# Two token tiles in one PSUM bank in a projection chunk of 256 columns of a decoder step

## The chip, the cores and the metric

The kernel runs on one core of a Trainium2 chip. Its time is device time in microseconds for one execution of the whole program, two decoder layers. The engines are TensorE (PE, matmuls and transposes into PSUM), ScalarE (ACT), VectorE (DVE), GpSimd (POOL, which here also issues the indirect DMAs, the gathers) and SyncE (SP, which issues the other DMAs). PSUM is held as eight banks of 128 partitions by 512 fp32 words.

## The reference

One step of a two-layer decoder for 512 prompt tokens and for 64 tokens of eight samples that have a paged cache. Each layer projects the input once, gives the columns to three groups of heads, and ends in a feed-forward block:

```python
def layer(x, pos, past, w, lam_init, past_len):
    z = x @ w['w_in']
    ca, cg, nq, ck, cv, sk, sv, wk, wv, gt, dq, dk, dv = jnp.split(z, _split_points(), axis=-1)
    ...
    y_conv, new_conv = conv_mixer(ca, cg, conv_buf, ...)
    ...
    o_nsa = gate[0] * o_cmp + gate[1] * o_sel + gate[2] * o_win
    ...
    o_diff = diff_mixer(dq, dk_all, dv_all, pos, dk_pos, lam, w['diff_subln_g'], lam_init)
    mix = jnp.concatenate([y_conv, o_nsa, o_diff], axis=-1) @ w['w_out']
    x = layer_norm(DN_ALPHA * x + mix, w['ln1_g'], w['ln1_b'])
    h = jax.nn.silu(x @ w['ffn_w1']) * (x @ w['ffn_w3'])
    return layer_norm(DN_ALPHA * x + h @ w['ffn_w2'], w['ln2_g'], w['ln2_b']), ...
```

The columns that matter here are `nq` (the queries of the sparse attention, 512 columns) and `dv` (the values of the differential attention, 256 columns), the last two chunks that a layer projects. (Lines marked "..." and the arguments of the mixers are cut.)

## The kernel before

The 576 tokens lie as four prompt tiles of 128 tokens and one samples' tile of 64. Matrices are kept as a high and a low part, and a product is the sum of three matmuls (high by high, high by low, low by high; `product`, L358). For the samples' tile high and low parts are stacked as 128 rows, so it takes two matmuls and one addition of its two halves afterwards.

`chunk` (L558) projects N columns of `w_in` at a time through `dense_tok` (L374). A chunk reads `w_in` in eight weight tiles kt of 128 rows: load by SP (L181), split into high and low by ACT (L187) and DVE (L190), then the five token tiles m. Weight tiles 0 to 5 run as steps in which all five token tiles are served; the last two are kept, and token tile by token tile is finished with them and handed on: samples first, then prompt tiles 0 to 3. Each token tile sums up in a PSUM bank of its own. The banks go by tags, of which there are a fixed number (`PBUFS`, L148): a0 and a1 two each, t1 two, h one and t0 one:

```python
acc = [PS(b) for b in ("a0", "a0", "a1", "a1", last)]
...
for m in (4, 0, 1, 2, 3) if last == "t0" else range(5):
```

In a chunk `last` is "t0": the samples' tile lies in the one bank t0. When a token tile is done, `evac` (L559) copies it from PSUM into an H slot (`cp`, L213, in this stage on ACT) and calls the chunk's sink. `sink_q` (L636) rotates the queries and transposes them on PE (L649) through bank t0. `sink_e` (L591) copies the values with POOL (L593) and stores them.

The chunks run in the order d, c, q, e (`ORDER`), so the chunk of `dv`, called e here, follows the queries' chunk. It has N = 256; the others have 512 or 280. Beside them run the operands of the differential attention (`diff_operands`, L852, transposes L866) and parts of the samples' branch (`spe`, L1103 to L1124). After the chunks come the prompts' attention (`diff_scores`, L872, whose scores sum up in bank a0; `diff_turn`, L891) and the samples' (`keys_T`, L1142, transposes of gathered keys; `sample_diff_av`, L1281, products with gathered values; L985 and L1214 are transposes of attention weights).

Working tiles come from 30 U slots and 26 H slots; `W` gives the one that was freed longest ago, and a load into a slot waits for its last reader. The program is written as streams that `merge` (L124) deals out by planned costs, and a list scheduler then sets the order on each engine by its own estimate of times and by what each instruction depends on. So a dependency that changes can move instructions far from it.

Of the kernel before, what the change touches and what calls it, by code (L numbers as in the profile page):

```python
# [135 lines left out]
def kernel(ctx: ExitStack, tc: tile.TileContext, a: dict, o: dict, nlayers: int = DEPTH):  # L136
# [27 lines left out]
    def free(*ts, lag=0):  # L164

        for t in ts:
            _, tag, i = owner.pop(id(t))
            since[tag][i] = next(clock) + lag

    def T(tag, shape, dt=F):  # L170
        return sb.tile(shape, dt, tag=tag, name=f"{tag}_{next(uid)}", bufs=1)
# [5 lines left out]
    def PS(tag, dt=F):  # L177
        return ps.tile([128, 512], dt, tag=tag, name=f"{tag}_{next(uid)}", bufs=PBUFS[tag])

    def load(out, in_):  # L180
        nc.sync.dma_start(out, in_)  # L181
# [4 lines left out]
    def act(out, in_, func=AF.Copy, **kw):  # L186
        S.activation(out, in_, func, **kw)  # L187
# [13 lines left out]
    def split(h, l, x, eng=None):  # L201

        act(h, x)
        return sub(l, x, h.bitcast(F), eng)
# [8 lines left out]
    def cp(out, in_):  # L213

        if next(turn) % ratio[0] == 1:
            return V.tensor_copy(out, in_)  # L216
        return S.activation(out, in_, AF.Copy)  # L217
# [8 lines left out]
    def mm(out, lhsT, rhs, start, stop):  # L226
        return PE.matmul(out, lhsT, rhs, start=start, stop=stop)  # L227

    def wait_for(ins, *others):

        for x in others:
            tc.add_manual_dep(ins.ins, x.ins.name, mybir.DependencyInfo(mybir.DependencyClass.Sync, mybir.DependencyReason.DATA), reason="together")
# [8 lines left out]
    first = T("first", [128, NFIRST])  # L241
# [120 lines left out]
    def product(out, s_, wh, wl, first, last):  # L362


        if not isinstance(s_, tuple):
            mm(out, s_, wh, first, False)
            mm(out, s_, wl, False, last)
        else:
            hs, ls = s_
            mm(out, hs, wh, first, False)  # L370
            mm(out, hs, wl, False, False)
            mm(out, ls, wh, False, last)

    def dense_tok(w_rows, KT, N, st, sink, tail=0, last="h", done=None, raws=None, nh=8):  # L374


        acc = [PS(b) for b in ("a0", "a0", "a1", "a1", last)]

        def weights(kt, wh, wl):
            if raws and kt in raws:  # L380
                raw = raws[kt]
            else:
                raw = W("H", [128, N])
                load(raw, w_rows(kt))
            split(wh, wl, raw)
            free(raw)

        def step(kt, m, wh, wl):
            first, last = kt == 0, kt == KT - 1
            out = acc[m][:, :N]  # L390
            product(out, st(kt, m), wh, wl, first, last)

        for kt in range(KT - tail):
            wh, wl = own = [W("H", [128, N], FR) for _ in range(2)]
            weights(kt, wh, wl)
            for m in range(5):
                step(kt, m, wh, wl)
            free(*own)
            if done:
                done(kt)  # L400
            yield N * 14 / 2400
        res = []
        for kt in range(KT - tail, KT):
            if len(res) < nh:
                own = [W("H", [128, N], FR) for _ in range(2)]
                wh, wl = own
            else:
                own = [W("U", [128, 2, N], FR)]
                wh, wl = own[0][:, 0], own[0][:, 1]
            weights(kt, wh, wl)  # L410
            res.append((kt, wh, wl, own))
        for m in (4, 0, 1, 2, 3) if last == "t0" else range(5):
            for kt, wh, wl, _ in res:
                step(kt, m, wh, wl)
            sink(m, acc[m])
            yield 0.6 + N * len(res) * 2.8 / 2400
        for kt, _, _, own in res:
            free(*own)
            if done:
                done(kt)  # L420
# [34 lines left out]
    def layer(l, x, x_src, raws):  # L455
# [100 lines left out]
            return tuple(x[part][kt // 2][:, kt % 2, c0:c0 + R] for part in range(2))  # L556

        def chunk(c0, N, sink, raws=None):  # L558
            def evac(m, acc):  # L559
                z = W("H", [128 if m < 4 else NS, N])  # L560
                if m < 4:
                    cp(z, acc[:, :N])
                    sink(m, 128, z)
                else:
                    act(z, acc[64:128, :N])
                    add(z, acc[0:64, :N], z)
                    sink(m, NS, z)
                free(z, lag=LAG)

            yield from dense_tok(lambda kt: w_in[kt * 128:(kt + 1) * 128, c0:c0 + N], 8, N, st_x, evac, tail=TAIL, last="t0", raws=raws, nh=NH)  # L570
# [933 lines left out]
        for kt in range(8):  # L1504
            small = kt < 3
            parts = [[W("H", [128, 512], FR) for _ in range(2)] if small else W("U", [128, D], FR) for _ in range(2)]
            for c in range(2):
                wh, wl = (t[c] if small else t[:, c * 512:(c + 1) * 512] for t in parts)
# [6 lines left out]
        st = st_of(mix)  # L1515
        ln.fetch(0)
        for m in range(5):
            if m < 4:
                ln.fetch(m + 1)
            acc = [PS("a0"), PS("a1")]  # L1520
# [48 lines left out]
        for c in range(2):  # L1569
            def sink(m, acc):  # L1570
                ln.add(m, c, acc)
                if c:
                    ln.finish(m)
# [61 lines left out]
```

## Time and profile before

| | us |
|---|---|
| median of 3 runs | 2069.74 |
| lowest and highest | 2063.65 and 2074.16 |
| the profiled execution, its own time | 2071.4 |
| its span | 2069.6 |

The page of the profile gives the busy time of each engine and its share of the span; the trace behind it has every instruction with its start, its duration and what ended the idle time ahead of it. A row of a timeline reads: start, duration, engine, line, operation, output tile <- input tiles, shape, number of instructions taken together, and in brackets the idle time just before and what released the engine. In names of tiles, a, t and h are PSUM banks (a0 and a1 both read a), H and U are slots, `in_...` are tensors in DRAM, and `first` is the identity that PE transposes by. The mean granted clock of PE is 0.969 of full speed over the run.

### The profile page before, as it was taken

To read this page: it belongs to the slowest core of one execution; us is meant where nothing else is said; L and a number is where in the kernel's file an instruction comes from. 1 tells how busy PE (TensorE), PEld (TensorE's weight loads), DVE (VectorE), ACT (ScalarE), POOL (GpSimd) and SP (SyncE) were. 2 spreads that over 40 slices of the span, in tenths; PEclk is the share of its full clock that TensorE was granted. 3 is DMA by queue.
4 is the path that set the end of the run, shared out by engine and by line. 5 is a ranking of instruction groups with operands and counts; after the bars stand their busy time and mean duration, and the time that the engine had idled before them with its cause. 6 is when DMAs were issued, how large, how long until landed. Compare 5 with 4: busy or idle time off the path is not lost. (4 is left out here: it accounts for less than half of the span.)

```text
span 2069.6 us, 32882 instructions
## 1 busy us (share of the span) xinstructions
PE 1933.5 (93%) x12222; PEld 1631.7 (79%) x12222; DVE 1101.2 (53%) x3012; ACT 916.7 (44%) x2368; POOL 206.7 (10%) x233
## 2 busy tenths in 40 slices
PE   8999888989999999999999997989899999999997
PEld 6887765656689999988879776656566899999885
DVE  3568476866573333323456665678666633333236
ACT  3635565767422333321245545667673223333211
POOL 2011022121010000000120110221110000000002
PEclk9999899999999999999999998999999999999999
DMA  6423143243423332352153321441433332324411
GB/s 200 137 76 103 28 145 128 83 146 99 136 92 117 97 122 83 93 187 77 48 174 108 96 71 45 152 155 57 138 108 118 112 122 82 122 84 130 149 56 51
DMA packets 190252, 223.91 MB, mean 108 GB/s; under 512 B 19092, under 2 KB 138812, under 8 KB 189948
## 3 DMA queue, kind: packets, MB, share of 16 engines
q1 hardware_dynamic: 171660, 154.69, 24.5%
q0 software_dynamic: 18432, 67.12, 10.2%
q8 instruction: 97, 1.59, 0.3%
q14 instruction: 63, 0.52, 0.1%
HBM read 206.23 MB, written 24.15 MB: 111 GB/s over the span
## 5 line engine op out<-in xcount | busy, mean ns | idle before, releaser
L227 PE MATMUL a<-H,U 128*128 128x512 f32 (+3 forms) x2264 | 552.8, 411 | 14.0 <-ACT H L187 11.6
L190 DVE TENSOR_TENSOR H<-H,H 128x512 fp32r<-128x512 f32 (+5 forms) x392 | 255.5, 657 | 510.5 <-ACT H L187 482.8
L227 PEld LDWEIGHTS a<-H,U 128*128 128x128 f32 (+1 forms) x2264 | 386.2, 190 | 111.2 <-issue 15.4
L187 ACT ACTIVATE H<-H 128x512 fp32r<-128x512 f32 (+4 forms) x418 | 240.8, 583 | 519.9 <-DMA H<-in_ffn_w_dram 298.8
L227 PE MATMUL a<-U,H 128*128 128x288 f32 (+2 forms) x3008 | 399.2, 306 | 7.9 <-DMA U<-in_cache_diff_v_dram,idx 6.7
L227 PEld LDWEIGHTS a<-U,H 128*128 128x128 f32 (+1 forms) x3008 | 370.2, 181 | 21.7 <-DMA U<-in_cache_diff_v_dram,idx 7.3
L227 PE MATMUL t<-U,H 128*128 128x288 f32 x1584 | 288.7, 297 | 0.4 <-ACT U L187 0.4
L227 PEld LDWEIGHTS t<-U,H 128*128 128x128 f32 x1584 | 243.5, 190 | 1.0 <-ACT U L187 0.6
L227 PE MATMUL a<-U,U 128*128 128x512 f32 (+4 forms) x744 | 200.7, 379 | 7.9 <-ACT H L187 3.7
L227 PE MATMUL h<-U,U 128*128 128x257 f32 (+5 forms) x708 | 152.4, 376 | 13.1 <-ACT U L217 13.0
L217 ACT ACTIVATE U<-t 64x256 f32<-64x256 f32 (+4 forms) x393 | 142.8, 366 | 45.6 <-PE t L757 24.5
L227 PEld LDWEIGHTS a<-U,U 128*128 128x128 f32 x744 | 129.4, 191 | 34.2 <-ACT U L187 7.4
L227 PEld LDWEIGHTS h<-U,U 128*128 128x128 f32 (+1 forms) x708 | 114.6, 185 | 40.3 <-ACT U L217 17.3
L227 PE MATMUL h<-U,H 128*128 128x288 f32 x528 | 140.9, 296 | 0.0
L187 ACT ACTIVATE U<-H 128x288 fp32r<-128x288 f32 (+4 forms) x160 | 64.4, 438 | 143.8 <-DVE H L190 104.1
L217 ACT ACTIVATE H<-t 128x512 f32<-128x512 f32 (+1 forms) x172 | 94.9, 564 | 45.6 <-PE t L1145 23.5
L547 DVE SCALAR_TENSOR_TENSOR U<-U,cw,U 128x512 f32<-128x512 f32 x240 | 109.4, 510 | 0.1
L227 PEld LDWEIGHTS h<-U,H 128*128 128x128 f32 x528 | 99.3, 188 | 0.0
L190 POOL TENSOR_TENSOR U<-U,U 128x512 f32<-128x512 f32 x24 | 33.6, 1417 | 599.1 <-DVE rs_u L321 459.9
L187 ACT ACTIVATE U<-t 128x256 fp32r<-128x256 f32 (+4 forms) x132 | 47.1, 370 | 97.0 <-PE t L350 40.8
L190 DVE TENSOR_TENSOR U<-H,U 128x64 fp32r<-128x64 f32 (+6 forms) x204 | 69.9, 385 | 31.1 <-ACT U L187 24.8
L216 DVE COPY H<-t 128x512 f32<-128x512 f32 (+1 forms) x92 | 57.2, 626 | 45.7 <-PE t L1214 15.6
(293 smaller groups left out, 2268.9 us busy)
## 6 DMA issues: line engine op xcount, KB each, us to landing
H<-in_ffn_w_dram SPq DMA_DIRECT2D x264, 256.0 KB
H<-in_w_in_dram SPq DMA_DIRECT2D x64, 256.0 KB
H<-in_w_out_dram SPq DMA_DIRECT2D x32, 256.0 KB
xd<-U SPq DMA_DIRECT2D x24, 256.0 KB
U<-xd SPq DMA_DIRECT2D x12, 512.0 KB
U<-in_x_prompt_dram SPq DMA_DIRECT2D x8, 512.0 KB
H<-in_state_nsa_win_v_dram SPq DMA_DIRECT2D x16, 256.0 KB
H<-in_state_nsa_win_k_dram SPq DMA_DIRECT2D x16, 256.0 KB
```

The lines of the kernel that those rows point to most:

```text
L187: S.activation(out, in_, func, **kw)
L190: return (eng or V).tensor_tensor(out, x, y, op=op)
L216: return V.tensor_copy(out, in_)
L217: return S.activation(out, in_, AF.Copy)
L227: return PE.matmul(out, lhsT, rhs, start=start, stop=stop)
L547: V.scalar_tensor_tensor(out=ac, in0=ex, scalar=wc, in1=ac, op0=OP.mult, op1=OP.add)
```

## The change

It concerns chunks with 2N <= 512, and that is chunk e alone, once in each layer. Its four prompt tiles lie two in a bank: tiles 0 and 1 in the two halves of the first a0, tiles 2 and 3 in those of the second. The samples' tile takes a bank a1; bank t0 and the other a1 are not used by this chunk any more. The flag that starts a sum is set for the first tile of a bank only, and the second tile's first matmul is made to come after it. The copies of a pair are made after the last matmul of the pair's second tile. Nothing else is written differently; every instruction stays, and in each layer 16 matmuls, one ACT and one DVE instruction name an a bank where they named t.

```diff
--- before.py
+++ after.py
@@ -363,18 +363,24 @@
 
 
         if not isinstance(s_, tuple):
-            mm(out, s_, wh, first, False)
-            mm(out, s_, wl, False, last)
+            i = mm(out, s_, wh, first, False)
+            j = mm(out, s_, wl, False, last)
         else:
             hs, ls = s_
-            mm(out, hs, wh, first, False)
+            i = mm(out, hs, wh, first, False)
             mm(out, hs, wl, False, False)
-            mm(out, ls, wh, False, last)
+            j = mm(out, ls, wh, False, last)
+        return i, j
 
     def dense_tok(w_rows, KT, N, st, sink, tail=0, last="h", done=None, raws=None, nh=8):
 
 
-        acc = [PS(b) for b in ("a0", "a0", "a1", "a1", last)]
+        if 2 * N > 512:
+            acc = [PS(b) for b in ("a0", "a0", "a1", "a1", last)]
+        else:
+            acc = [t[:, c * 256:(c + 1) * 256] for t in (PS(b) for b in ("a0", "a0", "a1")) for c in range(2)]
+
+        starts = {}
 
         def weights(kt, wh, wl):
             if raws and kt in raws:
@@ -386,9 +392,15 @@
             free(raw)
 
         def step(kt, m, wh, wl):
-            first, last = kt == 0, kt == KT - 1
+
+            first, last = kt == 0 and (2 * N > 512 or m % 2 == 0), kt == KT - 1 and (2 * N > 512 or m in (1, 3, 4))
             out = acc[m][:, :N]
-            product(out, st(kt, m), wh, wl, first, last)
+            i, j = product(out, st(kt, m), wh, wl, first, last)
+            if 2 * N <= 512 and kt == 0:
+                if m % 2:
+                    wait_for(i, starts[m - 1])
+                starts[m] = i
+            return j
 
         for kt in range(KT - tail):
             wh, wl = own = [W("H", [128, N], FR) for _ in range(2)]
@@ -411,8 +423,13 @@
             res.append((kt, wh, wl, own))
         for m in (4, 0, 1, 2, 3) if last == "t0" else range(5):
             for kt, wh, wl, _ in res:
-                step(kt, m, wh, wl)
-            sink(m, acc[m])
+                j = step(kt, m, wh, wl)
+            if 2 * N > 512 or m == 4:
+                sink(m, acc[m])
+            elif m % 2:
+
+                sink(m - 1, acc[m - 1], j)
+                sink(m, acc[m])
             yield 0.6 + N * len(res) * 2.8 / 2400
         for kt, _, _, own in res:
             free(*own)
@@ -556,10 +573,12 @@
             return tuple(x[part][kt // 2][:, kt % 2, c0:c0 + R] for part in range(2))
 
         def chunk(c0, N, sink, raws=None):
-            def evac(m, acc):
+            def evac(m, acc, after=None):
                 z = W("H", [128 if m < 4 else NS, N])
                 if m < 4:
-                    cp(z, acc[:, :N])
+                    i = cp(z, acc[:, :N])
+                    if after:
+                        wait_for(i, after)
                     sink(m, 128, z)
                 else:
                     act(z, acc[64:128, :N])
```

The scheduler gives another order. In the chunk e of layer 0, on PE (a is the bank of a token tile, H_482 to H_497 the halves of a weight tile, high and low; U_24 to U_30 the prompts' x, U_32 the samples'), the samples' products of weight tiles 0 to 3 (H_484 to H_494) stood behind prompt tile 0's of weight tile 4 (H_496, H_497) before:

```order
L227 MATMUL a_482_2569<-H_493_2631,U_29_123 128x256
L227 MATMUL a_479_2566<-H_496_2651,U_26_120 128x256
L227 MATMUL a_479_2566<-H_497_2652,U_26_120 128x256
L227 MATMUL a_479_2566<-H_496_2651,U_30_124 128x256
L227 MATMUL t_483_2570<-H_484_2571,U_32_126 128x256
L227 MATMUL t_483_2570<-H_485_2572,U_32_126 128x256
L227 MATMUL t_483_2570<-H_487_2591,U_32_126 128x256
L227 MATMUL t_483_2570<-H_488_2592,U_32_126 128x256
L227 MATMUL t_483_2570<-H_490_2611,U_32_126 128x256
```

and now stand with the weight tile that they belong to:

```order
L227 MATMUL a_480_2567<-H_482_2569,U_24_118 128x256
L227 MATMUL a_480_2567<-H_483_2570,U_24_118 128x256
L227 MATMUL a_480_2567<-H_482_2569,U_28_122 128x256
L227 MATMUL a_481_2568<-H_483_2570,U_32_126 128x256
L227 MATMUL a_479_2566<-H_485_2589,U_24_118 128x256
L227 MATMUL a_480_2567<-H_485_2589,U_24_118 128x256
L227 MATMUL a_481_2568<-H_485_2589,U_32_126 128x256
L668 MATMUL t_444_2388<-first_63,H_439_2370 128x128 x4
L885 MATMUL t_477_2554<-first_63,U_472_2535 128x128 x4
```

The samples' products of the first weight tile have moved ahead of those of the second weight tile, and so on for each.

Some 75 instructions later, on PE, the transposes of the gathered keys of sel_k (L1145, in the new file L1164) and a score of 512 columns (a_612, now a_610). Before:

```order
L866 MATMUL t_568_2916<-first_63,U_562_2885 128x128 x4
L227 MATMUL a_612_3047<-U_474_2541,U_473_2540 128x512
L227 LDWEIGHTS ident_b_103
L227 MATMUL a_612_3047<-causal_b_105,ident_b_103 128x128
L895 MATMUL t_576_2939<-first_63,H_518_2768 128x128
L1145 MATMUL t_545_2833<-first_63,U_539_2821 128x128 x4
L1145 MATMUL t_547_2840<-first_63,U_540_2823 128x128 x4
```

and now:

```order
L885 MATMUL t_566_2914<-first_63,U_560_2883 128x128 x4
L1164 MATMUL t_543_2831<-first_63,U_537_2819 128x128 x4
L1164 MATMUL t_545_2838<-first_63,U_538_2821 128x128 x4
L227 MATMUL a_610_3045<-U_474_2541,U_473_2540 128x512
L227 LDWEIGHTS ident_b_103
L227 MATMUL a_610_3045<-causal_b_105,ident_b_103 128x128
L914 MATMUL t_574_2937<-first_63,H_516_2766 128x128
```

The transposes of keys have moved ahead of the score. On POOL the gather for the first of them (U_539, now U_537) has moved ahead of the last of the three copies of `sink_e` before it.

In layer 0, among the gathers that POOL issues in the attention, before (U_1139 and U_1140 are the pair of gathers of diff_v that `sample_diff_av` uses together):

```order
L313 DMA U_1119_4876<-in_cache_diff_v_dram,idx_15_92 128x1024
L313 DMA U_1120_4878<-in_cache_diff_v_dram,idx_15_92 128x1024
L313 DMA U_1139_4959<-in_cache_diff_v_dram,idx_15_92 128x1024
L313 DMA U_1140_4961<-in_cache_diff_v_dram,idx_15_92 128x1024
L313 DMA U_1184_5119<-in_cache_nsa_sel_k_dram,idx_91 128x1024
L313 DMA U_1270_5466<-in_cache_diff_k_dram,idx_15_92 128x1024
```

and now:

```order
L313 DMA U_1117_4874<-in_cache_diff_v_dram,idx_15_92 128x1024
L313 DMA U_1118_4876<-in_cache_diff_v_dram,idx_15_92 128x1024
L313 DMA U_1182_5117<-in_cache_nsa_sel_k_dram,idx_91 128x1024
L313 DMA U_1137_4957<-in_cache_diff_v_dram,idx_15_92 128x1024
L313 DMA U_1138_4959<-in_cache_diff_v_dram,idx_15_92 128x1024
L313 DMA U_1268_5464<-in_cache_diff_k_dram,idx_15_92 128x1024
```

A gather of sel_k has moved ahead of the pair. On PE, the first use of this pair and what followed, before:

```order
L997 MATMUL t_1147_4995<-first_63,H_911_4086 128x128
L227 MATMUL a_1118_4875<-U_1139_4959,H_1142_4968 64x256
L227 MATMUL h_4867<-H_1148_4997,H_58_241 128x128 x2
L1418 MATMUL t_1158_5045<-first_63,U_722_3404 128x128 x2
L985 MATMUL t_1163_5067<-first_63,U_1125_4906 128x128 x2
L985 MATMUL t_1163_5067<-first_63,U_1126_4907 128x128 x2
L227 MATMUL a_1118_4875<-U_1140_4961,H_1142_4968 64x256
L227 MATMUL a_1118_4875<-U_1139_4959,H_1142_4968 64x256
```

and now (the pair is U_1137 and U_1138):

```order
L227 MATMUL h_4865<-H_1142_4973,H_297_1612 64x256 x2
L1016 MATMUL t_1145_4993<-first_63,H_909_4084 128x128
L227 MATMUL h_4865<-H_1146_4995,H_58_241 128x128 x2
L1437 MATMUL t_1156_5043<-first_63,U_720_3402 128x128 x2
L1004 MATMUL t_1161_5065<-first_63,U_1123_4904 128x128 x2
L1004 MATMUL t_1161_5065<-first_63,U_1124_4905 128x128 x2
L227 MATMUL a_1116_4873<-U_1137_4957,H_1140_4966 64x256
L1004 MATMUL t_1176_5106<-first_63,U_1123_4904 128x128 x2
L1004 MATMUL t_1176_5106<-first_63,U_1124_4905 128x128 x2
L227 MATMUL a_1116_4873<-U_1138_4959,H_1140_4966 64x256
```

The products into h and the transposes L1418 and L985 have moved ahead of the pair's first product, and the next transposes of L985 ahead of its second. Between these places layer 0 has more such moves from about 384 to 470 us of the trace of before; layer 1 has only single ones.

## Rows read from the trace of the kernel before

**Rows 1.** Page, part 1: busy time, share of the span, instructions

```profile
PE 1933.5 (93%) x12222; PEld 1631.7 (79%) x12222; DVE 1101.2 (53%) x3012; ACT 916.7 (44%) x2368; POOL 206.7 (10%) x233
```

**Rows 2.** Busy time by stretch: from:to, us, engines, PE's clock, DMA share, GB/s

```profile
252.00:282.40 30.40, 25.57 (x163) 24.21 (x163) 12.96 (x37) 14.37 (x39) 4.01 (x5) 0.75 0.32 87
1275.50:1305.90 30.40, 24.98 (x156) 23.62 (x157) 12.91 (x37) 15.23 (x38) 3.34 (x4) 0.74 0.28 80
384.00:470.00 86.00, 75.37 (x566) 53.48 (x566) 61.43 (x229) 59.67 (x189) 15.34 (x19) 0.94 0.35 111
448.00:460.00 12.00, 9.29 (x39) 5.44 (x39) 2.91 (x9) 4.43 (x15) 1.87 (x2) 0.57 0.51 175
```

**Rows 3.** PE's waits, 252 to 282.4: us in total, times, longest

```profile
PE a L227 <- ACT H L187: 3.1, 2, 2.5
PE t L227 <- DVE spe L1103: 0.9, 1, 0.9
```

**Rows 4.** Timeline of SP, 255 to 275 us

```profile
263.31 2.19 SPq L181 DMA_DIRECT2D H<-in_w_in_dram  x2
...
271.48 0.38 SPq L181 DMA_DIRECT2D H<-in_w_in_dram  x1
```

**Rows 5.** Timeline of ACT, 262 to 290 us

```profile
267.54 0.42 ACT L187 ACTIVATE H<-H 128x256 fp32r<-128x256 f32 x1
...
281.24 0.39 ACT L217 ACTIVATE H<-a 128x256 f32<-128x256 f32 x1 [0.33 <-PE a L227]
281.95 0.39 ACT L217 ACTIVATE H<-a 128x256 f32<-128x256 f32 x1 [0.33 <-PE a L227]
282.39 0.60 ACT L217 ACTIVATE U<-t 128x512 fp32r<-128x512 f32 x1
```

**Rows 6.** Timeline of PE, 252 to 290 us

```profile
252.12 1.22 PE L227 MATMUL a<-H,U 128*128 128x256 f32 x4 [0.60 <-ACT H L187]
...
254.70 2.75 PE L227 MATMUL a<-H,U 128*128 128x256 f32 x12
257.29 0.60 PE L649 MATMUL t<-first,H 128*128 128x128 f32 x4
...
259.81 1.21 PE L227 MATMUL a<-H,U 128*128 128x256 f32 x8
261.92 0.41 PE L227 MATMUL t<-spe,cst 128*128 128x64 f32 x2 [0.91 <-DVE spe L1103]
...
268.01 1.22 PE L227 MATMUL a<-H,U 128*128 128x256 f32 x4 [2.55 <-ACT H L187]
...
269.74 4.95 PE L227 MATMUL a<-H,U 128*128 128x256 f32 x23
274.52 1.11 PE L227 MATMUL t<-H,U 128*128 128x256 f32 x8
275.47 1.23 PE L227 MATMUL a<-H,U 128*128 128x256 f32 x9
...
283.04 0.66 PE L866 MATMUL t<-first,U 128*128 128x128 f32 x4 [0.37 <-ACT U L217]
...
287.11 0.49 PE L227 MATMUL a<-U,U 128*128 128x512 f32 x1 [0.52 <-ACT H L187]
...
288.19 1.09 PE L1145 MATMUL t<-first,U 128*128 128x128 f32 x8 [0.27 <-DMA U<-in_cache_nsa_sel_k_dram,idx]
```

**Rows 7.** Timeline of POOL, 278 to 292 and 425 to 470 us

```profile
281.30 2.48 POOL L593 TENSOR_SCALAR U<-H 128x256 f32<-128x256 f32 x3
283.95 1.00 POOL L313 DMA_INDIRECT U<-in_cache_nsa_sel_k_dram,idx  x1 [0.17 <-PE a L227]
...
442.77 0.94 POOL L313 DMA_INDIRECT U<-in_cache_diff_v_dram,idx  x1 [13.13 <-PE t L1214]
```

**Rows 8.** Timeline of PE, 438 to 460 us

```profile
440.56 1.95 PE L227 MATMUL a<-U,H 128*64 128x256 f32 x16 [0.17 <-ACT H L217]
...
449.81 1.11 PE L227 MATMUL a<-U,H 128*64 128x256 f32 x2 [2.99 <-DMA U<-in_cache_diff_v_dram,idx]
...
454.45 3.25 PE L227 MATMUL a<-U,H 128*64 128x256 f32 x13
```

## The prediction

> **What bounds the kernel now.** I read the page first: TensorE is busy for 93% of the span, no other engine for more than 53% [rows 1]. So a matmul that is taken away, or a gap of PE that is filled, shortens the kernel; a gap on another engine does not. The change takes no matmul away: both orders hold the same instructions, and per layer 16 matmuls and two copies name another bank. It can only move gaps of PE and the stretches in which its clock is low. The next view is therefore the busy time by stretch [rows 2]. Chunk e of layer 0 runs from 252.0 to 282.4 us: PE is busy for 25.57 of 30.40 us at a granted clock of 0.75. Layer 1 has the same stage at 1275.5, with 24.98 us and 0.74, so each number found for layer 0 is counted twice.
>
> What ends PE's waits there stands in the list of waits [rows 3]: 3.1 us on ACT's split of a weight tile (L187), in two waits of which one is 2.5, and 0.9 us on the samples' branch (spe). No wait in it is for the bank that the samples' tile shares with the transposes of q. The scheduler has put the samples' matmuls behind those transposes, so the sharing costs order, not a wait. The 2.5 us wait is read along its chain. SP starts two loads of w_in tiles from 263.31 on, the second in the last 0.33 of the row's 2.19 us, and a third only at 271.48 [rows 4]; ACT splits the second at 267.54 [rows 5]; PE goes on at 268.01 [rows 6]. SP's order is the same in both kernels, and the slots that these loads write into were held by q's rows, which the transposes free. That chain stays.
>
> **The change part by part.**
>
> 1. *Samples' matmuls ahead of the wait.* Before, all 16 stand behind 268 us: 8 at 274.52, 2 and 4 later, 2 last. After, the four of weight tiles 0 and 1 run before the wait for weight tile 2, and those of tiles 2 and 3 with their own weights (first pair of order rows). Up to the transposes at 257.29, 17 chunk matmuls stand where 16 stood. The twelve at 254.70 have a pitch of (257.29 - 254.70) / 12 = 0.216 us, so these transposes slip by 0.22. The next run has 11 matmuls for 8 at 259.81, that is 3 x 0.216 = 0.65 more, inside the 0.91 us for which PE waits at 261.92; if that cover is gone they cost 0.65, less what is saved below. From 268.01 on 84 of the chunk's matmuls are left instead of 88 (4 + 23 + 8 + 9 in the rows and 44 behind them); eight of them at 274.52 take until 275.47, a pitch of 0.119, so 4 x 0.119 = 0.48 us are saved at the end of the chunk [rows 6]. If the slip is passed on through q's transposes to the weight loads, the net is 0.22 - 0.48 = -0.26 per layer. Bounds: -0.48 (nothing passed on) and +0.22 (all passed on and nothing gained). I take -0.26, since the transposes at 257.29 are of the same tiles whose slots the loads wait for; **-0.5** for two layers.
>
> 2. *Copies in pairs.* Before, ACT copies each prompt tile 0.33 us after its last matmul, while PE fills the next bank: the last one at 281.95 for 0.39, and at 282.39 it turns to the copy for which PE then waits 0.37 us, at 283.04 [rows 5, 6]. After, tile 2 is copied only once tile 3 is done, so behind the last matmul two copies stand and not one. ACT's next copy starts 0.39 later, and PE is already waiting for it: +0.39 per layer, bounds 0 (ACT has slack that the chain does not show, or PE's next scores move ahead) and +0.39. I take the upper end, because the wait is there already; **+0.8** for two layers. A tile read while its bank partner is being written is what the scheduler avoids here.
> The Trainium skill, page "PSUM — Partial Sum Buffer", section "PSUM bank collisions raise a hardware error", says that two engines may not touch one bank in the same partitions at once, even in different columns, while different banks run clean. It speaks against a shared bank: by it a pair's copies cannot start under the partner's matmuls, which gives this term's +0.39 per layer; without it the term would be 0. Of the trace of before only the second half can be seen, and it agrees: ACT's copy at 281.24 [rows 5] runs while PE fills another bank, as the next copy's wait for PE shows.
>
> 3. *Sample key transposes ahead of a 512-column score* (second pair of order rows). They wait for a gather of sel_k, issued at 283.95, right behind three copies on POOL of 2.48 / 3 = 0.83 us each [rows 7]. On POOL the gather now stands ahead of the third of these copies, so it can go at about 283.1 and land 0.83 earlier. Before, PE waits 0.52 us ahead of the score at 287.11 and 0.27 ahead of the transposes at 288.19 [rows 6]; in the new order the transposes would find their data at 288.19 - 0.83 = 287.4, against a score that starts at 287.11 now. The score then follows them, with its own wait covered: 0 is what I take. Bounds per layer: -0.8 (both waits, 0.52 + 0.27, are covered) and +1.1 (the row of the 8 transposes, 1.09 us, falls wholly into the path of the score and of the softmax behind it). Two layers: 0, from -1.6 to +2.2.
>
> 4. *Layer 0 from 384 to 470 us.* Here the order of prompts and samples is dealt out anew: PE is busy for 75.37 of 86.00 us [rows 2], so 10.6 us are open. The largest gap is 2.99 us at 449.81, on a gather of diff_v that POOL issued at 442.77, 7.04 us before [rows 7, 8]. The clock is low after it: 0.57 from 448 to 460, with PE busy for 9.29 us [rows 2], so 9.29 x (1 - 0.57) = 4.0 us are lost there. After, POOL has a gather of sel_k ahead of this pair (third pair of order rows), which pushes the pair back; but PE also comes to the pair later: the block of products and transposes that stood between its first product and the others, from 449.81 + 1.11 to 454.45 or 3.5 us [rows 8], now stands ahead of the first (last order rows). Push and cover are of one size. Bounds: -7.0, if gap and low clock go (2.99 + 4.0), and +3.5, if the pair's gathers take half as long again as their 7.04, being second and third of three and not first and second. I take 0, the 3.5 of cover against the 3.5 of push.
>
> The sum is -0.5 + 0.8 + 0 + 0 = +0.3 us. Against the profiled execution's own 2071.4 that is 2071.7; that execution lies 1.7 above the median of 2069.74, so on the median the forecast is **2070.0**. The bounds add up to -0.96 - 1.6 - 7.0 = -9.6 and 0.44 + 0.78 + 2.2 + 3.5 = +6.9.
>
> **The rivals.** The bound of what a measurement can tell is 0.5%, or 10.3 us; the three runs of before alone spread over 10.5.
>
> A, the forecast: every gain is hidden behind the chain of transposes, slots and weight loads, and the time stays. For it: PE's waits in the stage have other causes than the bank. Against it: the new order in layer 0. Chance 0.76.
>
> B: the gap on diff_v and the low clock behind it vanish, since PE comes to the pair later. 2069.7 - 7.0 = 2062.7 us, still within 0.5%. For it: the 3.5 us block that now stands ahead of the pair is longer than the gap of 2.99. Against it: the pair is issued behind another gather. Chance 0.08.
>
> C, the slower side: the gather of sel_k that now stands ahead of the pair waits on POOL for a slot, and the pair behind it is issued late. Decisive is whether it is held for more than the 7.04 us that the pair took in all; at that point PE stands still for 7.0 us more and runs another stretch at the low clock, 4.0 us: +11.0, or 2080.7. For it: POOL stood still for 13.13 us ahead of the issue at 442.77 [rows 7], so waits of that length occur there. Against it: the scheduler put the gather there because it reckoned with a free slot. Chance 0.06.
>
> D, the faster side: with the chunk's matmuls spread more evenly ahead of the waits, the clock doesn't fall in chunk e. In layer 0 25.57 us of work ran at 0.75, so 25.57 x 0.25 = 6.4 would come back, 12.8 in two layers: 2057. Against it: the 2.55 us wait before 268.01 stays, and one matmul more ahead of it is little. Chance 0.05.
>
> E, the change doesn't do what it says: the samples' matmuls stay behind the transposes for another reason, and the time is that of before, 2069.7. The order speaks against it; the gain would be nil anyway. Chance 0.05.
>
> **How the numbers follow.** The likeliest case gives 2070.0. A and B and E together hold 0.89; the range from 2062 to 2077 takes in B at its lower end and A's upper bound of 2069.7 + 6.9, and leaves out C and D, 0.11, and some of the spread of single runs. Faster by over 0.5% is D, 0.05; slower by over 0.5% is C, 0.06; the rest, 0.89, is the same.
>
> **What would show it.** Step 1: in the trace of after, four samples' matmuls before 262 us, the wait on the split of weight tile 2 still about 2.5 us, and the last matmul of the chunk 0.3 us earlier relative to the stage's start. Step 2: two copies by ACT back to back behind that last matmul, and PE's wait ahead of the next transposes at 0.4 to 0.8. Step 3: the gather of sel_k issued about 0.8 earlier. Step 4: the span from 384 to the same place near 470 within 3.5 us of the 86.0. The forecast is wrong if the stage's clock rises to 0.9, if a gather of layer 0 is late by more than 7 us, or if the new order reaches beyond these stretches, which I have priced at nothing.

## The result, and the profile after

The changed kernel is slower. Over 17 runs each its median is 2077.74 us (2070.03 to 2083.92) against 2066.24 (2057.23 to 2074.16) for the kernel before; the ratio is 1.0058 with a 95% interval of 1.0044 to 1.0072. That is 11.5 us more, where no change had been forecast (2070.0, at most 2077.0). The profiled execution of the changed kernel took 2077.33 us with a span of 2075.6; that of before, 2071.4, lies 5 us above the median of its 17 runs, so the two traces are only 6 us apart and single stretches must be compared over several traces.

The page shows the same work as before [rows 1]. The busy sum of PE does not tell where 11 us went:

```profile
PE 1932.2 (93%) x12222; PEld 1629.0 (78%) x12222; DVE 1102.0 (53%) x3012; ACT 915.2 (44%) x2368; POOL 205.0 (10%) x233
```

So the two traces were laid side by side by work: a boundary stands, in each run, where PE has done the same amount of it (each instruction counted with its usual pitch in the trace of before). These are stretches of the changed kernel, columns as in [rows 2]: chunk e of layer 0, the stretch behind it, and from there three that answer to 365 to 405, 405 to 432 and 432 to 500 us of before; then 365 to 601 (the end of layer 0's attention) as a whole, and the layer 1 stretch from 1392 to 1625.

```profile
251.81:283.04 31.23, 25.41 (x174) 23.46 (x173) 13.97 (x42) 16.52 (x45) 5.92 (x8) 0.83 0.37 102
283.04:310.70 27.66, 24.24 (x165) 15.72 (x165) 25.17 (x72) 21.70 (x67) 8.42 (x10) 1.00 0.54 172
364.10:406.96 42.86, 37.93 (x288) 27.12 (x288) 31.58 (x132) 30.69 (x108) 2.42 (x5) 0.92 0.22 75
406.96:438.44 31.48, 26.41 (x186) 19.53 (x185) 20.91 (x80) 20.39 (x62) 5.75 (x6) 0.89 0.31 100
438.44:507.00 68.56, 60.19 (x437) 38.95 (x436) 44.67 (x133) 45.68 (x134) 12.66 (x14) 0.95 0.37 117
364.10:608.98 244.88, 218.59 (x1454) 155.78 (x1454) 160.07 (x510) 141.71 (x410) 29.63 (x33) 0.95 0.34 111
1396.29:1629.59 233.30, 213.58 (x1448) 153.59 (x1448) 156.52 (x494) 140.58 (x404) 29.62 (x30) 0.96 0.35 114
```

The same stretches of the kernel before:

```profile
251.21:283.96 32.75, 27.08 (x174) 25.27 (x173) 14.01 (x42) 16.68 (x45) 5.67 (x8) 0.75 0.34 94
283.96:310.83 26.87, 24.54 (x166) 15.87 (x165) 25.39 (x72) 21.84 (x67) 8.94 (x10) 1.00 0.55 182
364.33:404.94 40.61, 35.96 (x266) 25.70 (x266) 32.46 (x133) 29.72 (x103) 2.36 (x5) 0.92 0.24 81
404.94:431.99 27.05, 25.00 (x216) 18.54 (x215) 19.65 (x79) 21.45 (x69) 5.71 (x6) 1.00 0.33 107
431.99:499.97 67.98, 59.86 (x429) 39.35 (x429) 43.91 (x132) 45.25 (x131) 12.72 (x14) 0.92 0.39 122
364.33:600.86 236.53, 214.91 (x1454) 153.49 (x1453) 159.05 (x510) 141.63 (x410) 29.57 (x33) 0.96 0.36 115
1391.84:1624.80 232.96, 212.23 (x1449) 153.28 (x1449) 156.43 (x494) 140.65 (x404) 29.46 (x30) 0.97 0.36 114
```

Chunk e, which the change is about, is 1.5 us shorter in this pair of traces, but that is no more than the spread: in the ten traces with the old chunk in layer 0 (the kernel before, e2, e4, e6 and e9 to e14 below) it took from 31.51 to 32.75 us, and in the four with the new chunk (the changed kernel, e1, e3, e5) from 31.23 to 32.60. The stretch behind it is 0.8 longer. The loss is in layer 0 from 365 to 601 us, 244.88 against 236.53, with the same 1454 matmul records in it; the largest piece in this pair of traces, 4.4 of 8.4 us, is the stretch 405 to 432, where PE sat still for 31.48 - 26.41 = 5.1 us instead of 2.05, and the clock, full before, was 0.89. Layer 1 shows next to nothing.

What is late in that stretch stands on POOL. Before, the timeline of POOL has the four gathers of diff_k for one pair of samples at 410.70, 411.94, 419.27 and 420.51 us. This is the third of them:

```profile
419.27 0.94 POOL L313 DMA_INDIRECT U<-in_cache_diff_k_dram,idx  x1 [6.38 <-PE t L1145]
```

After:

```profile
408.00 0.94 POOL L313 DMA_INDIRECT U<-in_cache_diff_k_dram,idx  x1 [3.29 <-PE a L227]
409.25 0.94 POOL L313 DMA_INDIRECT U<-in_cache_diff_k_dram,idx  x1 [0.30 <-DVE sfr L1158]
427.06 1.06 POOL L313 DMA_INDIRECT U<-in_cache_diff_k_dram,idx  x1 [16.88 <-DVE U L222]
428.43 0.94 POOL L313 DMA_INDIRECT U<-in_cache_diff_k_dram,idx  x1 [0.30 <-DVE H L1370]
```

The first two go 2.7 us earlier; the samples' work runs ahead of the prompts' there. The third waits for 16.88 us and the fourth follows it. In both kernels these two are written into two U slots that hold attention weights of the prompts, and the transposes that read these (L985, in the new file L1004) come later now. PE then waits for both (timeline of PE after):

```profile
431.13 0.66 PE L1164 MATMUL t<-first,U 128*128 128x128 f32 x4 [1.24 <-DMA U<-in_cache_diff_k_dram,idx]
...
433.53 1.97 PE L1164 MATMUL t<-first,U 128*128 128x128 f32 x8 [1.31 <-DMA U<-in_cache_diff_k_dram,idx]
```

Before, PE waited 1.3 us in all for these gathers, 0.7 at the longest.

### The profile page after: what moved, and what is told of

It is laid out like the page before. It is cut to its first block, busy times and chain, and to the rows that moved or that the text cites. A ratio compares the mean times of both kernels' runs of the same rounds, so it can differ in the third digit from the quotient of the medians.

```text
span 2075.6 us, 32875 instructions
## 1 busy us (share of the span) xinstructions
PE 1932.2 (93%) x12222; PEld 1629.0 (78%) x12222; DVE 1102.0 (53%) x3012; ACT 915.2 (44%) x2368; POOL 205.0 (10%) x233
```

## The experiments

All were timed in the same way beside the kernel before on the same chip. Many of them lay down an issue order. This is the code for it, at the end of the kernel, with a table QUEUES of places in the order in which each engine's instructions are written down; the edges set the order on one engine and make nothing wait for another:

```diff
     assert not owner, len(owner)
+    traced = {}
+    for i in nc.cur_bb.bb.instructions:
+        traced.setdefault(i.engine, []).append(i)
+    for name, pieces in QUEUES.items():
+        mine = traced[getattr(mybir.EngineType, name)]
+        row = [mine[k] for first, n in pieces for k in range(first, first + n)]
+        for p, q in zip(row, row[1:]):
+            tc.add_manual_dep(q, p.name, mybir.DependencyInfo(mybir.DependencyClass.NoSync, mybir.DependencyReason.DATA), reason="queue")
```

The results, with the length of 365 to 601 us (layer 0) from one trace of each kernel:

| kernel | ratio to before | 95% interval | 365 to 601, us |
|---|---|---|---|
| before | | | 236.53 |
| the changed kernel | 1.0058 | 1.0044 to 1.0072 | 244.88 |
| e1 new chunk, old order | 0.9999 | 0.9984 to 1.0014 | 236.46 |
| e2 old chunk, new order | 1.0057 | 1.0037 to 1.0077 | 245.10 |
| e3 layer 0 alone | 1.0070 | 1.0047 to 1.0092 | 246.27 |
| e4 layer 1 alone | 1.0058 | 1.0039 to 1.0077 | 238.68 |
| e5 after, late slots | 1.0045 | 1.0026 to 1.0065 | 241.83 |
| e6 new order, old POOL | 1.0078 | 1.0053 to 1.0102 | 245.10 |
| e7 own bank, no pairs | 1.0025 | 1.0005 to 1.0045 | 238.91 |
| e8 pairs alone | 1.0054 | 1.0033 to 1.0076 | 248.61 |
| e9 layer 1 alone, late slots | 1.0064 | 1.0042 to 1.0086 | 237.22 |
| e10 new order to 372 us | 1.0004 | 0.9985 to 1.0023 | 231.79 |
| e11 new order from 372 us | 1.0046 | 1.0029 to 1.0062 | 245.47 |
| e12 new order, 365 to 405 | 1.0037 | 1.0022 to 1.0052 | 239.30 |
| e13 new order, 405 to 500 | 1.0042 | 1.0022 to 1.0061 | 245.60 |
| e14 new order, 365 to 432 | 1.0037 | 1.0019 to 1.0056 | 245.65 |

The last column is of one execution each, and some of these lie far from the median of their kernel: e7's took 2084.86 us (median 2072.80), e14's 2081.65 (median 2072.46). With the order of before in this stretch (before, e1, e4, e7, e9, e10) the column runs from 231.79 to 238.91; with the changed kernel's order in 405 to 432 (the changed kernel, e2, e3, e6, e8, e11, e13, e14), from 244.88 to 248.61. These two groups are clearly apart; differences of a few us inside a group say nothing.

**The chunk or the order: e1 to e4.** e1 is the changed kernel with the table of the kernel before for everything behind chunk e in both layers; e2 is the kernel before with the changed kernel's table for layer 0. e3 and e4 make the change in one layer:

```diff
-        if 2 * N > 512:
+        if not (2 * N <= 512 and pair[0]):
...
     def layer(l, x, x_src, raws):
+        pair[0] = l == 0
```

(and in the other places of the diff alike; l == 1 for e4).

> Chunk e with two tiles in a bank, in both layers, and behind it on PE, ACT, DVE and POOL the issue order of the kernel before, laid down by edges that make no engine wait for another. Theory 'order' (the loss is the new issue order of layer 0 from 384 to 470 us, the chunk itself gains): 0 to 3 us faster than before, about 2064. Theory 'bank' (the loss is in the shared banks: copies that wait for the partner, banks that come free later, about 5 to 6 us in each layer): 8 to 12 us slower than before, about 2077, as the changed kernel.

> Chunk e as before, in five banks, and behind it in layer 0 alone the issue order of the changed kernel. Theory 'order': 9 to 13 us slower than before, about 2077. Theory 'bank': within 2 us of before, about 2066.

> The change in layer 0 alone. Theory 'order': 10 to 13 us slower than before, the whole loss of the changed kernel. Theory 'bank': half the loss, 5 to 6 us slower.

> The change in layer 1 alone, where only single instructions change places behind the chunk. Theory 'order': 0 to 2 us faster than before. Theory 'bank': the other half of the loss, 5 to 6 us slower.

e1 takes the time of before, and e2, in which no bank is shared, the time of the changed kernel. These are e1's and then e2's stretches for 405 to 432 and 365 to 601:

```profile
403.04:429.86 26.82, 25.01 (x216) 18.54 (x215) 19.65 (x79) 21.48 (x69) 5.71 (x6) 1.00 0.34 109
362.42:598.88 236.46, 214.94 (x1453) 155.09 (x1453) 159.13 (x510) 141.74 (x410) 29.56 (x33) 0.96 0.35 115
```

```profile
406.22:439.30 33.08, 27.78 (x185) 20.36 (x184) 20.98 (x80) 20.42 (x62) 5.77 (x6) 0.85 0.30 96
363.60:608.70 245.10, 220.60 (x1453) 156.99 (x1453) 161.05 (x512) 142.33 (x410) 29.67 (x33) 0.94 0.34 111
```

The theory of the shared banks falls with these two: the loss goes with the order and not with the chunk. e3 carries all of it, as expected. e4 misses the expectation of the theory that stands: it had been thought to change only single places of layer 1, as the changed kernel does, but with layer 0 untouched the scheduler deals out layer 1 anew as well, and loses there nearly what the changed kernel loses in layer 0. Its stretch for 1392 to 1625, and its POOL at the same four gathers, now of layer 1:

```profile
1390.23:1630.65 240.42, 216.99 (x1448) 155.25 (x1448) 158.37 (x495) 141.41 (x404) 29.46 (x30) 0.96 0.34 111
```

```profile
1431.79 0.94 POOL L313 DMA_INDIRECT U<-in_cache_diff_k_dram,idx  x1 [6.28 <-PE a L227]
1433.04 0.93 POOL L313 DMA_INDIRECT U<-in_cache_diff_k_dram,idx  x1 [0.30 <-DVE U L190]
1450.86 1.07 POOL L313 DMA_INDIRECT U<-in_cache_diff_k_dram,idx  x1 [16.89 <-DVE U L222]
```

240.42 against 232.96, and the third gather waits 16.89 us here, 16.88 in layer 0 of the changed kernel. That made the gathers' slots the first suspect.

**Which half of the change: e7 and e8.** e7 undoes the pairs and moves the samples' tile into bank h; e8 keeps the pairs and leaves that tile in t0:

```diff
-            yield from dense_tok(..., tail=TAIL, last="t0", raws=raws, nh=NH)
+            yield from dense_tok(..., tail=TAIL, last="t0" if N > 256 else "h", raws=raws, nh=NH)
...
-        for m in (4, 0, 1, 2, 3) if last == "t0" else range(5):
+        for m in (4, 0, 1, 2, 3) if last == "t0" or N == 256 else range(5):
```

```diff
-            acc = [t[:, c * 256:(c + 1) * 256] for t in (PS(b) for b in ("a0", "a0", "a1")) for c in range(2)]
+            acc = [t[:, c * 256:(c + 1) * 256] for t in (PS(b) for b in ("a0", "a0")) for c in range(2)] + [PS("t0")]
```

> Before, with one edit: in chunk e the samples' tile lies in bank h and no longer in t0, and each prompt tile keeps its own bank. The samples' products are free of the queries' transposes as in the changed kernel, and the order in layer 0 from 384 to 470 us stays that of before. Theory 'order': 0 to 3 us faster than before, 2063 to 2066. If the earlier products of the samples were themselves what costs, by the slots of x or of the weights that they free earlier: 9 to 13 us slower.

> The other half of the change: the prompt tiles lie two in a bank, and the samples' tile stays in t0. In layer 0 the order behind the chunk from 384 to 470 us becomes the changed kernel's all the same, in layer 1 it stays that of before. Theories 'order' and 'slots': 9 to 13 us slower than before, 2075 to 2079. If the loss came with the samples' new bank: within 2 us of before.

e8 loses 0.54% with the samples' tile where it was: the pairs alone bring the new order of layer 0 and the loss. e7 keeps the old order there (238.91 us) and shows less than half of the loss, but it is not faster as expected: 0.25% slower, by an interval that nearly reaches 0 at one end and the changed kernel's interval at the other. What slows it is open. Earlier products of the samples gain nothing in either form.

**Slots and gathers: e5, e6, e9.** e5 is the changed kernel, e9 the kernel e4, both with two gathers of each layer in other slots; e6 is e2 with POOL in the order of before:

```diff
-        _, i = min((f, i) for i, f in enumerate(since[tag]) if f is not None)
+        _, i = (max if late else min)((f, i) for i, f in enumerate(since[tag]) if f is not None)
...
-                nat = [gather("cache_diff_k", l, 2 * p + s, hf) for s in range(2)]
+                nat = [gather("cache_diff_k", l, 2 * p + s, hf, p == 2 and hf == 1) for s in range(2)]
```

> The changed kernel, but in both layers the gathers of diff_k for the second half of the samples' pair p = 2 take the two slots that were freed last (by the first half's keys) and not the two that were freed longest ago (which hold attention weights of the prompts). Up to that gather in layer 0 the order is the changed kernel's. Theory 'slots' (the samples run ahead of the prompts in the new order, and these two gathers then wait for the prompts' transposes to give their slots up): the two gathers are issued at about 413 to 419 instead of 427.06 and 428.43 us, and most of the loss comes back: 0 to 4 us slower than before, 2066 to 2070. Theory 'pair' (the loss is the gather of sel_k that stands ahead of the pair of diff_v, rival C of the prediction): as the changed kernel, 9 to 13 us slower.

> Chunk e as before, and behind it in layer 0 the changed kernel's order on PE, ACT and DVE, but the order of before on POOL, where the pair of diff_v goes ahead of the gather of sel_k. Theory 'pair': the pair comes up to 7 us earlier and the loss falls to 2 to 6 us. Theory 'slots': POOL waits for the slots of the diff_k gathers all the same; 9 to 13 us slower than before, as with the changed kernel's order on all four engines.

> The change in layer 1 alone, with the two gathers of diff_k for the second half of the samples' pair p = 2 in the slots freed last. With the change in layer 1 alone and the old choice of slots those gathers waited 16.89 us on POOL and the stretch from 1392 to 1525 us of before grew from 133.1 to 141.5. Theory 'slots': the two gathers are issued within 10 us of the first two (at about 1440 and not 1450.86), the stretch takes 131 to 136 us, and the kernel is 0 to 5 us slower than before instead of 12. Theory 'order' alone (the new order costs whatever the gathers do): the stretch stays near 141 and the kernel 9 to 13 us slower.

e6 clears the gather of sel_k, rival C of the prediction: with the pair of diff_v ahead of it again, the loss is no smaller (0.78%). The pair itself was no earlier for it, since it waits for slots of its own:

```profile
453.89 0.94 POOL L319 DMA_INDIRECT U<-in_cache_diff_v_dram,idx  x1 [16.28 <-PE a L233]
```

It goes at 453.89 us here and at 453.04 in the changed kernel. So e6 doesn't show what a pair that is in time would be worth.

e5 and e9 bring the third gather of diff_k forward. POOL in e5, and in e9:

```profile
418.12 0.94 POOL L313 DMA_INDIRECT U<-in_cache_diff_k_dram,idx  x1 [6.66 <-PE t L1164]
420.02 0.94 POOL L313 DMA_INDIRECT U<-in_cache_diff_k_dram,idx  x1 [0.96 <-DVE rs_r L336]
438.13 0.94 POOL L313 DMA_INDIRECT U<-in_cache_diff_v_dram,idx  x1 [17.17 <-ACT U L187]
...
447.29 0.94 POOL L313 DMA_INDIRECT U<-in_cache_diff_v_dram,idx  x1 [6.99 <-PE a L227]
...
456.42 0.94 POOL L313 DMA_INDIRECT U<-in_cache_nsa_sel_k_dram,idx  x1 [6.95 <-PE a L227]
```

```profile
1435.34 0.94 POOL L313 DMA_INDIRECT U<-in_cache_diff_k_dram,idx  x1 [5.56 <-PE t L1170]
```

but the time did not come back: 0.45% in e5, which the runs cannot tell from the 0.58% of the changed kernel, and 0.64% in e9. In the trace of e5 the stretch 365 to 601 takes 3 us less than in the changed kernel. In e9 the stretch for 1392 to 1625 is as long as in e4:

```profile
1387.67:1627.89 240.22, 217.15 (x1449) 153.54 (x1448) 158.48 (x497) 141.19 (x405) 28.88 (x30) 0.96 0.34 111
```

In e5 the wait has only moved: the next gather, of diff_v, waits 17.17 us at 438.13. But neither kernel tests the slots by themselves. With other slots the dependencies change, and behind these gathers the scheduler deals out the attention once more: in e5 the pair of diff_v (447.29) stands ahead of the gather of sel_k (456.42), in the changed kernel behind it (453.04 and 451.35); in e9 a gather of diff_k (1479.91) stands behind the second gather of sel_k (1476.76), in e4 ahead of it (1481.88 and 1487.57). So e5 and e9 show that giving these gathers other slots is no cure; what the slots cost under a fixed order they don't show.

PE's own waits tell more. These are its waits for gathers of diff_k from 365 to 601 us, in all, how many and the longest, first in e6 and then in e7:

```profile
PE t L1151 <- DMA U<-in_cache_diff_k_dram,idx: 0.9, 1, 0.9
PE t L1145 <- DMA U<-in_cache_diff_k_dram,idx: 2.9, 2, 2.3
```

e6 loses the most of all kernels with 0.9 us of them, less than the 1.3 of the kernel before; e7, in the old order, has 2.9, more than the 2.5 of the changed kernel. PE's waits for these gathers do not carry the loss by themselves.

**Where in the order: e10 to e14.** All have chunk e of before and take the changed kernel's table for a part of layer 0 (e10 on PE, ACT and DVE only), the table of before for the rest:

> Chunk e as before; in layer 0 the changed kernel's order on PE, ACT and DVE from the chunk to about 372 us only, where the transposes of the gathered keys stand ahead of the score of 512 columns; the order of before from there on. Theory 'slots' (the loss is behind 372 us): 0.5 to 1.5 us more between 284 and 311, that is 0 to 3 us slower than before. If the early moves carry the loss: 6 us or more slower.

> The rest: chunk e and the order up to 372 us of layer 0 as before, the changed kernel's order on all four engines from there to 500 us. Theory 'slots': the third and fourth gathers of diff_k are issued about 8 us later than in before, the stretch from 365 to 500 us takes 7 to 9 us more, the kernel is 7 to 11 us slower. If the early moves carry the loss: within 4 us of before.

> Chunk e as before; in layer 0 the changed kernel's order only from about 365 to 405 us of before (the transposes of the convolution's output and of the gathered keys change places there), the order of before ahead of it and behind it, in both layers. If the loss lies in how far the samples have run ahead by 405 us, so that later gathers find their slots taken: 4 to 10 us slower than before. If the loss is made behind 405 us by the order there: within 3 us of before.

> The complement: the order of before up to about 405 us of layer 0, the changed kernel's order from there to 500 us. If the loss is made by the order behind 405 us: 6 to 11 us slower than before. If the samples' lead at 405 us is what costs: 0 to 4 us slower.

> The changed kernel's order from 365 to 432 us of layer 0, the order of before behind it. The stretch holds the late third and fourth gathers of diff_k (8 us later than in before) but not the pair of diff_v behind the gather of sel_k. If the diff_k gathers carry the loss: 7 to 11 us slower than before. If what follows them carries it: 0 to 4 us slower. If the loss is spread over many small waits: 3 to 7 us slower.

The early moves cost nothing that the runs can tell (e10), although their 0.9 us stand in the trace, 27.81 against 26.87:

```profile
284.06:311.87 27.81, 23.80 (x165) 15.61 (x164) 25.52 (x72) 21.91 (x67) 8.92 (x10) 1.00 0.55 180
```

The moves behind 372 us carry the loss (e11, 0.46%). It can't be cut further in two: 365 to 405 alone costs 0.37%, 405 to 500 alone 0.42%, and the whole no more that the runs can tell. e14's 0.37% (some 8 us, 4 to 12 by its interval) fits two of its expectations, the gathers of diff_k and many small waits. What the three share is a long stretch 405 to 432, here in e12, e13 and e14:

```profile
408.21:439.36 31.15, 27.60 (x194) 20.59 (x192) 21.69 (x81) 20.71 (x64) 5.65 (x6) 0.89 0.28 92
```

```profile
406.38:440.46 34.08, 27.14 (x206) 20.15 (x205) 19.71 (x78) 21.27 (x66) 5.76 (x6) 0.90 0.30 94
```

```profile
409.35:441.90 32.55, 27.43 (x189) 19.87 (x189) 21.30 (x80) 21.00 (x64) 5.76 (x6) 0.90 0.30 98
```

PE is still for 3.6, 6.9 and 5.1 us in it, against 2.05 before, and the clock is 0.89 or 0.90 instead of 1.00. In e12 the old order follows on a lead of the samples that it was not made for, and all four gathers of diff_k come some 5 us late, counted from 365 (the third at 426.74); in e13 and e14 the third comes at 428.73 and 429.45. But the stretch alone doesn't make the loss. In the trace of e7, whose order there is that of before, it is as long and the clock as low:

```profile
408.54:440.71 32.17, 28.20 (x216) 20.95 (x215) 19.94 (x79) 22.02 (x69) 5.71 (x6) 0.89 0.31 99
```

Over several traces the loss is spread. In the six kernels with the changed kernel's order from 372 to 500 us (the changed kernel, e2, e3, e6, e8, e11), 365 to 405 took 2.4 us more on average than in the six with the old order, 405 to 432 3.5 more and 432 to 500 3.6 more (69.8 against 66.2; the trace of before, with 67.98, is the longest of its group there).

What stays open is which moves of the order cost, and by which wait. The extra waits have no single cause: over the two groups of the table, PE waited from 365 to 601 us some 1.1 us more for gathers of diff_k on average, 0.6 for gathers of diff_v, 1.4 for ACT and 1.5 for DVE. The third gather is late in e11 to e14, but no run took its delay away and left the order as it was. Slots for all of the samples' gathers apart from the prompts' were not tried.

## Why the prediction was wrong, point by point

*What bounds the chunk.* Right. The chain of q's transposes, slots and weight loads stayed: the wait on the split of the third weight tile is still there, a little longer since PE comes to it earlier. PE after:

```profile
259.65 1.58 PE L227 MATMUL a<-H,U 128*128 128x256 f32 x11
...
267.86 1.01 PE L227 MATMUL a<-H,U 128*128 128x256 f32 x3 [3.17 <-ACT H L187]
```

*Terms 1 and 2*, -0.26 and +0.39 per layer, sum +0.13. e1, which holds these two alone, measures 0.9999 for two layers. The mechanism of term 2 is seen, the copies of a pair go back to back behind the second tile, with ACT waiting 0.76 for it:

```profile
279.35 0.66 ACT L217 ACTIVATE H<-a 128x256 f32<-128x256 f32 x2 [0.99 <-PE a L227]
280.77 0.66 ACT L217 ACTIVATE H<-a 128x256 f32<-128x256 f32 x2 [0.76 <-PE a L227]
```

but its price isn't: PE waits 0.18 at 281.48 and not at all at the transposes for which it waited 0.37 before [rows 6]. From the chunk's last row of products to these transposes it takes 1.76 us (280.22 to 281.98) against 1.64 (281.40 to 283.04), 0.1 more and not 0.39. (The 0.33 us that the prediction puts between a tile's last matmul and its copy is ACT's idle time ahead of the copy [rows 5].) The Trainium skill, page "PSUM — Partial Sum Buffer", section "PSUM bank collisions raise a hardware error", says that two engines may not touch one bank in the same partitions at once. No run here tests it: ACT's wait of 0.76 is laid down by the change itself, whose `wait_for` puts a pair's copies behind the pair's last matmul, and not by the scheduler as the prediction has it. The +0.39 per layer that the prediction worked out did not show in the time.

*Term 3*, taken as 0, bounds -0.8 to +1.1 per layer. The mechanism was right and the size was off: the gather of sel_k was issued earlier (281.95 after), PE came to it earlier still and waited 1.73 us at 287.15 instead of 0.52 + 0.27. The stretch 284 to 311 grew by 0.8 in the changed kernel, 0.7 in e2 and 0.9 in e10; in these two the gather keeps its old place on POOL, so its earlier issue gained nothing that shows. The growth is in layer 0 only and near the upper bound for one layer.

*Term 4*, taken as 0, bounds -7.0 to +3.5. This is the step that failed. From 365 to 601 us, which takes in its 384 to 470, the loss measured 244.88 - 236.53 = 8.4 us in the changed kernel and 8.6 in e2. Two things in it were wrong. First, it priced the one large gap that the trace of before shows, at 449.81 on diff_v, as though the new order could only move that one. But the gap did about what was said of it, push and cover near each other:

```profile
459.05 1.11 PE L227 MATMUL a<-U,H 128*64 128x256 f32 x2 [2.29 <-DMA U<-in_cache_diff_v_dram,idx]
```

2.29 instead of 2.99; the loss is spread over 365 to 500 us, most of it in places where the trace of before shows no large gap. Second, its upper bound was half of one gather's time, while 86 us of layer 0 were in a new order. What the runs show in its place is a price of the order as a whole: some 4 us more of waits, spread over gathers, ACT and DVE, and as much more busy time of the same matmuls. Why this order costs it, move by move, stays open. Two of the prediction's own signs of being wrong came: the third gather of diff_k was 7.8 us late (427.06 against 419.27), and the order reached beyond the stretch that it priced, though the largest piece lay inside it.

*The rivals.* C was on the right side and near in size (+11.0 us, and +11.5 measured), with 0.06, but that was luck: sel_k did stand ahead of the pair, after 16.41 us of waiting on POOL, but PE waited less for the pair than before (2.29 us), and e6 shows that the place of sel_k costs nothing. B and D did not come. The clock in chunk e rose a little, to 0.79 to 0.83 in the four traces of layer 0 with the new chunk against 0.75 to 0.79 with the old one, at best a third of the way that D asks for, and e1, with the new chunk, gained nothing from it. E can be ruled out: the samples' products did move.

*The range.* Its upper end of 2077.0 came from adding bounds of single gaps, and the measured 2077.74 lies just above. It looks nearer than it is: the forecast starts from the median of three runs, 2069.74, and over 17 runs the kernel before has 2066.24. As a change, +11.5 us stands against a forecast of +0.3 and an upper bound of +6.9. The larger mistake is in the chances: 0.06 for slower by over 0.5%. That the order of layer 0 was dealt out anew was known; that it would cost 8 us (and another new order 7.5 in layer 1, in e4) could have been read from nothing in the trace of before, so it should have had a wide range of its own on the slow side.

## What to carry to other kernels

Where a scheduler sets the order, an edit has two prices, its own and that of the new order, and the second can be the larger: lay the old order down on the new code and the new order on the old code, and each price is measured by itself. A gather that is 8 us late need not be the loss: compare what PE waits for it, in kernels with the loss and without it, before building on it. An edit that is to test one wait must leave the order as it is; where the scheduler deals again, as in e5 and e9, two things have changed. Where PE is 92% busy at full clock, as here from 405 to 432 us, a new order has 2 us of waits to take away and many to add: its range should reach much further on the slow side.

## What the runs showed of the hardware that was not expected

In a new order the same matmuls were busy for longer, beside the longer waits. From 365 to 601 us, over the eight kernels with the changed kernel's order in 405 to 432 (the changed kernel, e2, e3, e6, e8, e11, e13, e14), PE was still for 24.5 to 27.9 us, 26.3 on average, against 19.2 to 24.5, 21.9 on average, in the six with the old order (before, e1, e4, e7, e9, e10): 4.4 us more. The same matmuls were busy for 219.5 us on average instead of 214.7, 4.8 us more, at a granted clock of 0.94 or 0.95 instead of 0.95 to 0.98. Of the 9.2 us that the order costs there, the longer busy time is half.

The single traces do not tie the two together. These are e7, e5 and e12 from 365 to 601:

```profile
368.37:607.28 238.91, 214.45 (x1453) 155.53 (x1453) 159.52 (x511) 142.50 (x410) 29.85 (x33) 0.96 0.35 114
364.97:606.80 241.83, 218.97 (x1454) 155.81 (x1453) 160.29 (x512) 142.26 (x411) 29.06 (x33) 0.96 0.35 113
366.51:605.81 239.30, 217.60 (x1453) 156.71 (x1453) 160.76 (x512) 141.94 (x410) 29.57 (x33) 0.95 0.35 114
```

In e7 PE was still for 24.46 us, as long as in e2 (24.50), and busy for 214.45 against 220.60 there. In e12 it was still for only 21.70 us and busy for 217.60. In e5 it was busy for 218.97 us at a granted clock of 0.96, where the kernel before, at 0.96 too, was busy for 214.91. So longer waits came without longer busy time and the other way round, and in e5 the granted clock, to the two places shown, doesn't account for the busy time either. What does was not tested.
